# A decoder layer with woven attention: raised priority for the MLP's elementwise steps, and attention as one stream over the stages

## The chip, the cores and the metric

One core of a Trainium2 chip. The metric is the device time of one execution in microseconds. Two programs that compute the same thing are compared, one before and one after a change.

## The reference

One decoder layer on a sequence of 2048 tokens of width 1024, with a conditioning vector c. All inputs are float32.

```python
def reference(x, c, w_ada, b_ada, g_attn, w_in, b_f, sinks, w_out,
              g_mlp, w_up, conv_w, conv_b, w_down, g_final):
    mod = jax.nn.silu(c) @ w_ada + b_ada
    sh1, sc1, ga1, sh2, sc2, ga2 = jnp.split(mod, 6, axis=-1)
    for _ in range(DEPTH):
        h = modulate(rms_norm(x, g_attn), sh1, sc1)
        x = x + ga1[:, None, :] * hybrid_mixer(h, w_in, b_f, sinks, w_out)
        h2 = modulate(rms_norm(x, g_mlp), sh2, sc2)
        x = x + ga2[:, None, :] * conv_glu_mlp(h2, w_up, conv_w, conv_b, w_down)
    return rms_norm(x, g_final)
```

`modulate(h, shift, scale)` is h * (1 + scale) + shift. The mixer projects h once, runs eight heads of sliding-window attention (window 128, with ALiBi and a sink per head; "swa") and eight heads of causal forgetting attention over the whole prefix ("fox"), and projects both together. The MLP:

```python
def conv_glu_mlp(h, w_up, conv_w, conv_b, w_down):
    u = causal_dwconv(h @ w_up, conv_w, conv_b)
    a, g = jnp.split(u, 2, axis=-1)
    return (jax.nn.silu(g) * a) @ w_down
```

The inner width is 2816; the causal convolution has three taps.

## The kernel before, in words

The tokens are cut into four blocks n of 512. Every float32 product is made of three matmuls on a high and a low part (hh and hl, wh and wl): high by high, low by high, high by low. TensorE works on 128x128 weights against 512 columns (256 in parts of the attention).

For a block there are three pieces of program. `s1(n)` scales the rows of x by their RMS (`prep_tile`), transposes and modulates them (`lazy_h`) and makes q, k, v and the forget gates (products in lines L278, L611, L639). `s2(n)` is the attention of the block: scores s (L956), their running maximum mx (VectorE, L939), its transpose mt (L981) and m (L983), subtraction `t<-t,mm` (L1002), exponentials (ScalarE, L1007), the split into ph and pl (L716, L717), and the products with v (L1051, L1054). `s3(n)` is the rest:

1. the out-projection by rows (`rowmm`, L1171, operands yh, yl) in two halves of 512 columns. After each half, for each of four row tiles: gtmp = product times gate (L1245), x1row = x1row + gtmp (L1247), a store to x1_d (L1248) and the sum of squares (ScalarE, L487). After the second half the reciprocal root rs on GpSimd (L491, L492) and the scaling of both halves of the row by it on ScalarE (through `pscale`, L114, and at L1255);
2. the transposes of the scaled rows (L513), the modulation (hraw, L521, with mod and scl from the product of c and w_ada) and the split hh, hl (L114, L526). `lazy_h(rows, 8, 24, 2)` does this in two parts of 256 columns;
3. the up-projection (L1289) for 22 pairs of column tiles; a product lies in one of four PSUM tiles d. For each tile: u on ScalarE (L1319), two more taps on VectorE (L1322, L1325), the halo of the block before (L1330) and the halo for the next (ScalarE L1332, VectorE L1333), which is the last reader of the d tile. There are three u tiles. Then tanh (L1341), the product (L1342) and act (L1344);
4. the down-projection by rows (L1171, operands ah, al made by `get`, L1275 and L1276) in two halves, and the last RMS.

`merge(main, side, ratio)` weaves attention into the main work in program order: as main advances by some cost, the generator of the attention advances by ratio times that. A "B" event lets it fill a bubble, and "U" forces the fox heads of the block to be done. The stages are `s1(1)` and `s1(2)` with attention 0; `s3(0)` with attention 1; `s1(3)` and `s3(1)` with attention 2; `s3(2)` with attention 3; and `s3(3)` alone. `prime(n)` lets the first loads of an attention start in the stage before. The products of c with the later columns of w_ada (loads wada, L189; sums acc on VectorE, L201, L203) are spread over the first two stages.

The order of the instructions on each engine is set ahead of the run by a scheduler. It goes by program order as priority, and `tc.high_priority(offset=...)` moves the instructions inside it forward by so many places; among the instructions that it holds to be ready, the one with the best priority goes next. At run time every engine works through its queue strictly in that order, and DMAs are issued from SP's queue.

## Time and profile before

| | |
|---|---|
| time, median of 3 runs | 2670.57 us (2666.57 to 2671.02) |
| the profiled execution's own time | 2663.14 us |
| its span in the profile | 2661.4 us |
| mean granted TensorE clock | 0.976 |
| TensorE busy | 2544.1 us (96%), 12852 matmuls |
| VectorE, ScalarE, GpSimd busy | 1918.8, 1472.0, 91.7 us |
| HBM traffic | 588.24 MB in DMA packets, 220 GB/s over the span |

The profile shows one execution. Its times are in microseconds from the start of the span. A row of the waits names the waiting engine and line, then the engine, tile and line that ended the wait, then the sum, the count and the longest. A row of a timeline has start, duration, engine, line, operation, tiles written and read, shapes, count, and in brackets the idle time of that engine just before and what ended it. The letters are PE for TensorE (PEld for its weight loads), DVE for VectorE, ACT for ScalarE, POOL for GpSimd, SP for SyncE. Neighbouring instructions overlap a little, so eight in a row of 0.68 us each take less than eight times that.

### The profile page before, as it was taken

The page shows a single profiled execution, that of the slowest core. Times are in us where ns is not written, and L with a number is a line of the kernel's source. Part 1 is how long each engine was busy: PE and PEld are TensorE (multiplying, and loading weights), DVE is VectorE, ACT ScalarE, POOL GpSimd, SP SyncE. Part 2 cuts the span into 40 slices and gives each one's busy share as a digit, 9 for nine tenths or more (in the row PEclk, how much of TensorE's full clock was granted, in tenths as well). Part 3 has the DMA queues.
Part 4 walks back from the last instruction along what each step waited for, and adds up shares of the span by engine and source line. Part 5 has one row for each costly group of instructions (what it writes and reads, how often), then busy time and mean ns, then how long its engine had stood idle before and what let it go on. Part 6 is the DMA issues. An engine that isn't in the chain of part 4 may idle for free.

```text
span 2661.4 us, 38402 instructions
## 1 busy us (share of the span) xinstructions
PE 2544.1 (96%) x12852; PEld 2155.2 (81%) x12852; DVE 1918.8 (72%) x3813; ACT 1472.0 (55%) x3085; POOL 91.7 (3%) x171
## 2 busy tenths in 40 slices
PE   7999989799999999989999999799998999999998
PEld 5888888688887889878888888688877878888887
DVE  5568767799998668778888767888888876344433
ACT  4456665655667675575556665755555665421222
POOL 1001000100000010010000000100000000000000
PEclk9999999799999999999999999899998999999999
DMA  6967679576557876756666799365554577655564
GB/s 229 303 204 256 194 226 339 179 257 212 183 188 216 284 253 213 254 184 234 227 231 235 256 304 315 100 216 193 185 168 142 173 238 236 227 197 191 190 236 175
DMA packets 304769, 588.24 MB, mean 221 GB/s; under 512 B 32188, under 2 KB 137396, under 8 KB 304572
## 3 DMA queue, kind: packets, MB, share of 16 engines
q1 hardware_dynamic: 304572, 585.79, 65.8%
q8 instruction: 102, 1.67, 0.3%
q14 instruction: 95, 0.78, 0.1%
HBM read 440.95 MB, written 144.71 MB: 220 GB/s over the span
## 4 chain that ended last, share of the span: by engine, by line
PE 83%; DVE 5%; DMA 5%; ACT 4%; issue 2%; POOL 1%; SPq 1%; POOLq 0%; DVEq 0%; ACTq 0%
PE d L1289 36%; PE d L1171 21%; PE d L611 8%; PE s L956 4%; PE d L639 3%; PE o L1054 2%; PE o L1051 2%; PE d L278 1%; PE mb L988 1%; DVE t L1002 1%; PE s L786 1%; DMA yraw<-yd 1%; DMA q<-qd 1%; DMA wada<-in_w_ada_dram 1%; PE pt L828 1%
## 5 line engine op out<-in xcount | busy, mean ns | idle before, releaser
L1289 PE MATMUL d<-hh,wkh 128*128 128x512 f32 (+1 forms) x920 | 352.9, 386 | 13.4 <-DVE halo L1333 8.7
L1289 PE MATMUL d<-hl,wkh 128*128 128x512 f32 (+1 forms) x920 | 353.7, 386 | 0.0
L1289 PE MATMUL d<-hh,wkl 128*128 128x512 f32 (+1 forms) x920 | 352.5, 384 | 0.0
L381 DVE TENSOR_TENSOR wl<-wr,wh 128x1024 fp32r<-128x1024 f32 (+5 forms) x184 | 218.9, 1190 | 84.1 <-ACT wh L380 82.1
L973 ACT ACTIVATE t<-s,bc 128x256 f32<-128x256 f32 (+3 forms) x464 | 201.1, 483 | 135.7 <-PE s L956 72.0
L380 ACT CAST wh<-wr 128x1024 fp32r<-128x1024 f32 (+5 forms) x184 | 188.7, 1026 | 152.0 <-PE d L1289 62.8
L1319 ACT ACTIVATE u<-d,cb,cw 128x512 f32<-128x512 f32 x176 | 136.3, 777 | 207.7 <-PE d L1289 190.8
L716 ACT CAST ph<-t 128x512 fp32r<-128x512 f32 (+2 forms) x304 | 176.8, 590 | 119.3 <-PE o L1051 117.8
L1322 DVE SCALAR_TENSOR_TENSOR u<-d,cw,u 128x511 f32<-128x511 f32 x176 | 130.4, 743 | 150.7 <-ACT u L1319 149.6
L717 DVE TENSOR_TENSOR pl<-t,ph 128x512 fp32r<-128x512 f32 (+2 forms) x304 | 192.5, 644 | 31.5 <-ACT ph L716 31.2
L1289 PE MATMUL d<-hl,wh 128*128 128x512 f32 (+1 forms) x552 | 211.9, 385 | 0.0
L1289 PE MATMUL d<-hh,wh 128*128 128x512 f32 (+1 forms) x552 | 211.2, 384 | 0.4 <-ACT hh L114 0.4
L1289 PEld LDWEIGHTS d<-hh,wkh 128*128 128x128 f32 x920 | 173.9, 190 | 46.5 <-DVE halo L1333 9.3
L1289 PE MATMUL d<-hh,wl 128*128 128x512 f32 (+1 forms) x552 | 210.9, 383 | 0.0
L956 PE MATMUL s<-q,kkb 128*128 128x256 f32 (+2 forms) x1024 | 195.1, 309 | 7.3 <-ACT t L973 3.1
L1289 PEld LDWEIGHTS d<-hh,wkl 128*128 128x128 f32 x920 | 174.9, 190 | 32.0
L1289 PEld LDWEIGHTS d<-hl,wkh 128*128 128x128 f32 x920 | 174.9, 190 | 31.3 <-DVE hl L526 0.2
L1007 ACT ACTIVATE t<-t 128x512 f32<-128x512 f32 (+2 forms) x304 | 170.2, 601 | 13.0 <-DVE t L1006 10.1
L956 PEld LDWEIGHTS s<-q,kkb 128*128 128x128 f32 x1024 | 152.0, 194 | 19.9 <-ACT t L973 5.3
L1051 PE MATMUL o<-ph,vvb 128*128 128x256 f32 (+2 forms) x512 | 150.8, 310 | 10.0 <-ACT ph L716 3.6
L1054 PE MATMUL o<-pl,vvb 128*128 128x256 f32 (+2 forms) x512 | 146.7, 306 | 8.7 <-DVE pl L717 8.7
L611 PE MATMUL d<-hh,wh 128*128 128x512 f32 x360 | 142.0, 398 | 5.5 <-DVE lf L654 3.9
(232 smaller groups left out, 6078.9 us busy)
## 6 DMA issues: line engine op xcount, KB each, us to landing
wkh<-wsu SPq DMA_DIRECT2D x110, 512.0 KB, 3.3
wkl<-wsu SPq DMA_DIRECT2D x110, 512.0 KB, 4.2
wr<-in_w_up_dram SPq DMA_DIRECT2D x66, 512.0 KB, 4.8
wkh<-wsd SPq DMA_DIRECT2D x55, 512.0 KB, 3.9
wkl<-wsd SPq DMA_DIRECT2D x55, 512.0 KB, 4.3
wada<-in_w_ada_dram SPq DMA_DIRECT2D x96, 256.0 KB, 5.5
wr<-in_w_in_c_dram SPq DMA_DIRECT2D x45, 512.0 KB, 4.3
wsu<-wh SPq DMA_DIRECT2D x44, 512.0 KB, 2.9
```

What stands on the lines that cost most here:

```text
L380: nc.scalar.copy(wh, raw)
L381: nc.vector.tensor_sub(wl, raw, r32(wh))
L611: nc.tensor.matmul(ps, a[:, k, :], b[k], start=(k == 0 and i == 0), stop=(k == KT - 1 and i == 2),)
L716: nc.scalar.copy(ph[:, e0:], src[:, e0:])
L717: nc.vector.tensor_sub(pl[:, e0:], src[:, e0:], r32(ph[:, e0:]))
L956: nc.tensor.matmul(ps[:, o + low(c0) : o + w], st["kks"][kb // 4][:, (kb % 4) * P : (kb % 4 + 1) * P], qs[a][:, low(c0) : w], start=(a == ...
L973: nc.scalar.activation(tt[:, plain : o + w], ps[:, plain : o + w], AF.Identity, bias=bias(kb))
L1007: nc.scalar.activation(t1, t1, AF.Exp)
L1051: nc.tensor.matmul(po[:, c:], v, ph[:, o + c : o + w], start=(kb == 0), stop=False)
L1054: nc.tensor.matmul(po[:, c:], v, pl[:, o + c : o + w], start=False, stop=(kb == nkb - 1))
L1171: nc.tensor.matmul(acc[t], l[:, ts], r[:, k % 2, :], start=(i == 0 and l is ah and r is wh), stop=(i == n_k - 1 and l is al),)
L1289: nc.tensor.matmul(ps[:, c], w[a][:, k, :], b[k][:, c], start=(k == 0 and i == 0), stop=(k == KT - 1 and i == 2),)
```

## The change

It has four parts.

- `first()` raises the priority by 400 places for: the transposes and modulation of h2, the residual and RMS part after the second half of the out-projection, `get` (ah, al), the u and halo steps, and the gate.
- The scaling of rows by rs moves from ScalarE to VectorE: for block 0's x rows (8 instructions), and for the first half of the x1 rows (4 per block).
- The store of x1 follows the sum of squares in program order.
- The attention is one stream over the stages: the generator of the next attention is opened as soon as one ends, in the second and third stage also ahead of its own stage, and each stage's ratio is worked out from the attention still owed up to its block and the stage's length less 24. The priming hooks go.

```diff
+LEAD = 24.0
+AHEAD = 400
...
+    def first():
+        return tc.high_priority(offset=AHEAD)
...
-                a, b = h_pair(hh, hl, j)
-                ps = side_ps(w) if side else dense_ps(w)
-                transposes(ps, rows[part * nt : (part + 1) * nt], j)
-                modulate_one(a[:, c], b[:, c], ps, j, a0, s0)
+                with first() if parts == 2 else nullcontext():
+                    a, b = h_pair(hh, hl, j)
+                    ps = side_ps(w) if side else dense_ps(w)
+                    transposes(ps, rows[part * nt : (part + 1) * nt], j)
+                    modulate_one(a[:, c], b[:, c], ps, j, a0, s0)
...
-            pscale(r, r, rs)
+            if n == 0:
+                nc.vector.tensor_scalar(r, r, rs, None, ALU.mult)
+            else:
+                pscale(r, r, rs)
...
             for t in range(4):
-                tmp = tp.tile([P, 512], F32, tag="t", name="gtmp")
-                row = rows[t][half]
-                nc.vector.tensor_mul(tmp, r[t], gb)
-                adder = nc.vector
-                adder.tensor_add(row, row, tmp)
-                nc.sync.dma_start(x1_d[n][t * P : (t + 1) * P, cs], row)
-                if half == 0:
-                    sss.append(sums())
-                sumsq(row, sss[t][:, half : half + 1], tmp)
-                if half == 1:
-                    rs = rsqrt(sss[t])
-                    pscale(rows[t][0], rows[t][0], rs)
-                    nc.scalar.activation(tmp, row, AF.Copy, scale=rs)
-                    rows[t][1] = tmp
+                with first() if half == 1 else nullcontext():
+                    tmp = tp.tile([P, 512], F32, tag="t", name="gtmp")
+                    row = rows[t][half]
+                    nc.vector.tensor_mul(tmp, r[t], gb)
+                    nc.vector.tensor_add(row, row, tmp)
+                    if half == 0:
+                        sss.append(sums())
+                    sumsq(row, sss[t][:, half : half + 1], tmp)
+                    nc.sync.dma_start(x1_d[n][t * P : (t + 1) * P, cs], row)
+                    if half == 1:
+                        rs = rsqrt(sss[t])
+                        nc.vector.tensor_scalar(rows[t][0], rows[t][0], rs, None, ALU.mult)
+                        nc.scalar.activation(tmp, row, AF.Copy, scale=rs)
+                        rows[t][1] = tmp
...
+            with first():
+                if "h" in tails:
+                    ah, al = h_pair({}, {}, k, "t")
+                else:
+                    ah = tp.tile([P, TB], F32R, tag="t", name="ah")
+                    al = tp.tile([P, TB], F32R, tag="t", name="al")
+                nc.scalar.copy(ah, acts[k])
+                nc.vector.tensor_sub(al, acts[k], r32(ah))
...
+                with first():
+                    u = tp.tile([P, TB], F32, tag="u", name="u", bufs=3)
+                    c0, c1, c2 = (cw[t][:, ci : ci + 1] for t in range(3))
...
+            with first():
+                e = tp.tile([P, TB], F32, tag="t", name="e")
+                nc.scalar.activation(e, g, AF.Tanh, scale=0.5)
+                nc.vector.tensor_mul(a, a, g)
+                act = ap.tile([P, TB], F32, tag="act", name="act")
+                nc.vector.scalar_tensor_tensor(act, e, 1.0, a, ALU.add, ALU.mult)
...
+    stream = {"n": 0, "gen": None}
+
+    def attend(most):
+        while stream["n"] <= most:
+            if stream["gen"] is None:
+                stream["gen"] = s2(stream["n"])
+            try:
+                cost, need = next(stream["gen"])
+            except StopIteration:
+                fox_done.add(stream["n"])
+                stream["n"] += 1
+                stream["gen"] = None
+                continue
+            clock[0] += cost
+            stream["cost"] = stream.get("cost", 0.0) + cost
+            return cost, need
+        return None
+
+    def merge(main, n, length):
+
+        most = n if n in (0, NB - 1) else n + 1
+        begun = stream.get("cost", 0.0)
+        goal = sum(att_cost(i) for i in range(n + 1))
+        ratio = RM[n] * (goal - begun) / max(length - LEAD, 1.0)
         done_m = done_s = 0.0
         since, need = 1e9, 0.0
-        for main_event in main:
...
-                    spent += cost + (need if bubble else 0.0)
-                    clock[0] += cost
-                    since = 0.0
-                except StopIteration:
-                    side = None
-        if side is not None:
-            for cost, need in side:
-                clock[0] += cost
+            if isinstance(event, tuple) and event[0] == "U":
+                while n not in fox_done and stream["n"] <= n:
+                    got = attend(n)
+                    done_s += got[0] if got else 0.0
+            while spent < bubble or (done_s < done_m * ratio and since >= need):
+                got = attend(n if bubble > 1e6 else most)
+                if got is None:
+                    break
+                done_s += got[0]
+                need = got[1]
+                spent += got[0] + (need if bubble else 0.0)
+                since = 0.0
+        while stream["n"] <= n:
+            attend(n)
...
-    merge(s1(0), prologue_late(), 1.0)
-    merge(woven(chain(s1(1), s1(2)), late["extra"], 8), s2(0), RM[0] * att_cost(0) / 190.0)
-    merge(s3(0, [lambda: prime(2)]), s2(1), RM[1] * att_cost(1) / 383.0)
-    merge(chain(s1(3), s3(1, [lambda: yprep(2, 1), lambda: prime(3)])), s2(2), RM[2] * att_cost(2) / 478.0)
-    merge(s3(2, [lambda: yprep(3, 1)]), s2(3), RM[3] * att_cost(3) / 383.0)
-    merge(s3(3), None, 0.0)
...
+    merge(woven(chain(s1(1), s1(2)), late["extra"], 8), 0, 190.0)
+    merge(s3(0), 1, 383.0)
+    merge(chain(s1(3), s3(1, [lambda: yprep(2, 1)])), 2, 478.0)
+    merge(s3(2, [lambda: yprep(3, 1)]), 3, 383.0)
+    for event in s3(3):
+        clock[0] += event if not isinstance(event, tuple) else 0.0
```

The `with first():` blocks around u and the gate hold the same instructions as before.

How the order moves, at three places. In these rows the first number is the place in the engine's queue and a count stands at the end; lines of the changed kernel are some ten higher (L1322 becomes L1333, L1333 becomes L1344, L1002 becomes L1011).

VectorE late in the third block's up-projection, before:

```order
2649 L1061 TENSOR_TENSOR yo<-o,yo 64x256
2650 L1344 SCALAR_TENSOR_TENSOR act<-e,u 128x512
2651 L1322 SCALAR_TENSOR_TENSOR u<-d,cw_1138,u 128x511 x2
2652 L1325 SCALAR_TENSOR_TENSOR u<-d,cw_1128,u 128x510
2653 L1330 TENSOR_TENSOR u<-u,halo 128x2
2654 L1325 SCALAR_TENSOR_TENSOR u<-d,cw_1128,u 128x510
2655 L1330 TENSOR_TENSOR u<-u,halo 128x2
2656 L1002 TENSOR_TENSOR t<-t,mm 128x512 x7
2657 L1032 TENSOR_REDUCE rl<-lt 128x2
2658 L1342 TENSOR_TENSOR u<-u 128x512
2659 L933 TENSOR_TENSOR mx<-t 128x512
2660 L1333 SCALAR_TENSOR_TENSOR halo<-d,cw_1138,halo 128x1 x2
```

and after:

```order
2745 L1356 SCALAR_TENSOR_TENSOR act<-e,u 128x512
2746 L1333 SCALAR_TENSOR_TENSOR u<-d,cw_1150,u 128x511 x2
2747 L1336 SCALAR_TENSOR_TENSOR u<-d,cw_1140,u 128x510
2748 L1341 TENSOR_TENSOR u<-u,halo 128x2
2749 L1336 SCALAR_TENSOR_TENSOR u<-d,cw_1140,u 128x510
2750 L1341 TENSOR_TENSOR u<-u,halo 128x2
2751 L1011 TENSOR_TENSOR t<-t,mm 128x512 x5
2752 L1354 TENSOR_TENSOR u<-u 128x512
2753 L1011 TENSOR_TENSOR t<-t,mm 128x512 x2
2754 L1041 TENSOR_REDUCE rl<-lt 128x2
2755 L942 TENSOR_TENSOR mx<-t 128x512
2756 L1344 SCALAR_TENSOR_TENSOR halo<-d,cw_1150,halo 128x1 x2
```

Before, two u steps are followed by all their taps, then seven subtractions, then the two halos. After, at the place where this shape is left in this phase, five subtractions stand ahead of the product of the gate and two behind it, and the halos again come last.

VectorE at the start of the second block's up-projection, before:

```order
1611 L381 TENSOR_TENSOR wl<-wr,wh 128x1024
1612 L1322 SCALAR_TENSOR_TENSOR u<-d,cw_1138,u 128x511 x2
1613 L1325 SCALAR_TENSOR_TENSOR u<-d,cw_1128,u 128x510
1614 L1330 TENSOR_TENSOR u<-u,halo 128x2
1615 L983 TENSOR_REDUCE m<-mt 128x2
1616 L1325 SCALAR_TENSOR_TENSOR u<-d,cw_1128,u 128x510
1617 L1330 TENSOR_TENSOR u<-u,halo 128x2
1618 L381 TENSOR_TENSOR wl<-wr,wh 128x1024
1619 L1322 SCALAR_TENSOR_TENSOR u<-d,cw_1138,u 128x511
1620 L1342 TENSOR_TENSOR u<-u 128x512
1621 L933 TENSOR_TENSOR mx<-t 128x512
1622 L1333 SCALAR_TENSOR_TENSOR halo<-d,cw_1138,halo 128x1 x2
```

and after:

```order
1673 L386 TENSOR_TENSOR wl<-wr,wh 128x1024
1674 L1333 SCALAR_TENSOR_TENSOR u<-d,cw_1150,u 128x511 x3
1675 L1336 SCALAR_TENSOR_TENSOR u<-d,cw_1140,u 128x510
1676 L1341 TENSOR_TENSOR u<-u,halo 128x2
1677 L942 TENSOR_TENSOR mx<-t 128x512
1678 L1336 SCALAR_TENSOR_TENSOR u<-d,cw_1140,u 128x510
1679 L1341 TENSOR_TENSOR u<-u,halo 128x2
1680 L1011 TENSOR_TENSOR t<-t,mm 128x512 x6
1681 L1336 SCALAR_TENSOR_TENSOR u<-d,cw_1140,u 128x510
1682 L1341 TENSOR_TENSOR u<-u,halo 128x2
1683 L386 TENSOR_TENSOR wl<-wr,wh 128x1024
1684 L1344 SCALAR_TENSOR_TENSOR halo<-d,cw_1150,halo 128x1
```

Before, the first two halos stand behind a weight split (wl) and one maximum (mx); the subtractions come later. After, three u steps come at once, and six subtractions stand ahead of the weight split and the first halo.

VectorE at the third block's change from out- to up-projection, before:

```order
2303 L1245 TENSOR_TENSOR gtmp<-d,gb_17893 128x512 x4
2304 L1002 TENSOR_TENSOR t<-t,mm 128x512 x8
2305 L1061 TENSOR_TENSOR yo<-o,yo 64x256
2306 L1247 TENSOR_TENSOR x1row<-x1row,gtmp 128x512
2307 L933 TENSOR_TENSOR mx<-t 128x512
2308 L1247 TENSOR_TENSOR x1row<-x1row,gtmp 128x512 x3
```

and after:

```order
2330 L1255 TENSOR_TENSOR gtmp<-d,gb_18068 128x512 x4
2331 L1256 TENSOR_TENSOR x1row<-x1row,gtmp 128x512
2332 L1070 TENSOR_TENSOR yo<-o,yo 64x256
2333 L1041 TENSOR_REDUCE rl<-lt 128x2
2334 L1011 TENSOR_TENSOR t<-t,mm 128x512 x5
2335 L1256 TENSOR_TENSOR x1row<-x1row,gtmp 128x512
2336 L1011 TENSOR_TENSOR t<-t,mm 128x512 x2
2337 L942 TENSOR_TENSOR mx<-t 128x512
2338 L1256 TENSOR_TENSOR x1row<-x1row,gtmp 128x512 x2
2339 L1045 RECIPROCAL rl<-rl 128x2
2340 L1263 TENSOR_SCALAR x1row<-x1row,rs 128x512
```

Before, all four x1row sums stand behind eight subtractions. After, the first stands ahead of them, the second behind five, the last two behind seven, and the scaling of an x1row by rs has its place in VectorE's queue.

More of the change, by code (lines that the diff above doesn't have):

```diff
@@ L1079, in tile_decoder_layer @@
     clock = [0.0]
-    fox_done = [False]
+    fox_done = set()
     primed = {}
@@ L1099, in s2 @@
         held = []
-        fox_done[0] = False
         i = 0
@@ L1123, in s2 @@
                         groups = list(units[i]["groups"])
-                    fox_done[0] = i > n_fox
+                    if i > n_fox:
+                        fox_done.add(n)
             if len(held) > DEPTH or (held and not drained):
@@ L1269, in get @@
         def get(k):
-            if "h" in tails:
-                ah, al = h_pair({}, {}, k, "t")
-            else:
-                ah = tp.tile([P, TB], F32R, tag="t", name="ah")
-                al = tp.tile([P, TB], F32R, tag="t", name="al")
-            nc.scalar.copy(ah, acts[k])
-            nc.vector.tensor_sub(al, acts[k], r32(ah))
+            with first():
[6 more added lines that the diff above has]
+                nc.vector.tensor_sub(al, acts[k], r32(ah))
             return ah, al
@@ L1339, in s3 @@
                 next(extra, None)
-            e = tp.tile([P, TB], F32, tag="t", name="e")
-            nc.scalar.activation(e, g, AF.Tanh, scale=0.5)
-            nc.vector.tensor_mul(a, a, g)
-            act = ap.tile([P, TB], F32, tag="act", name="act")
-            nc.vector.scalar_tensor_tensor(act, e, 1.0, a, ALU.add, ALU.mult)
+            with first():
[4 more added lines that the diff above has]
+                nc.vector.scalar_tensor_tensor(act, e, 1.0, a, ALU.add, ALU.mult)
             acts.append(act)
@@ L1449, in chain @@
             yield from g
-    def merge(main, side, ratio):
+    stream = {"n": 0, "gen": None}
[19 more added lines that the diff above has]
+        ratio = RM[n] * (goal - begun) / max(length - LEAD, 1.0)
         done_m = done_s = 0.0
         since, need = 1e9, 0.0
-        for main_event in main:
-            bubble, cst = 0.0, main_event
-            if isinstance(cst, tuple):
-                bubble, cst = cst[1], 0.0
+        for event in main:
+            bubble, cst = 0.0, event
+            if isinstance(event, tuple):
+                bubble, cst = event[1], 0.0
             done_m += cst
@@ L1461, in merge @@
             spent = 0.0
-            if isinstance(main_event, tuple) and main_event[0] == "U":
-                while side is not None and not fox_done[0]:
-                    cost, need = next(side)
-                    done_s += cost
-                    clock[0] += cost
-            while side is not None and (
-                spent < bubble or (done_s < done_m * ratio and since >= need)
-            ):
-                try:
-                    cost, need = next(side)
-                    done_s += cost
-                    spent += cost + (need if bubble else 0.0)
-                    clock[0] += cost
-                    since = 0.0
-                except StopIteration:
-                    side = None
-        if side is not None:
-            for cost, need in side:
-                clock[0] += cost
+            if isinstance(event, tuple) and event[0] == "U":
[12 more added lines that the diff above has]
+            attend(n)
     def att_cost(n):
@@ L1505, in tile_decoder_layer @@
     late["extra"] = prologue_later()
-    merge(s1(0), prologue_late(), 1.0)
-    merge(woven(chain(s1(1), s1(2)), late["extra"], 8), s2(0), RM[0] * att_cost(0) / 190.0)
-    merge(s3(0, [lambda: prime(2)]), s2(1), RM[1] * att_cost(1) / 383.0)
-    merge(chain(s1(3), s3(1, [lambda: yprep(2, 1), lambda: prime(3)])), s2(2), RM[2] * att_cost(2) / 478.0)
-    merge(s3(2, [lambda: yprep(3, 1)]), s2(3), RM[3] * att_cost(3) / 383.0)
-    merge(s3(3), None, 0.0)
+    late_steps, since, need = prologue_late(), 0.0, 3.0
+    for event in s1(0):
+        cst = event if not isinstance(event, tuple) else 0.0
+        clock[0] += cst
+        since += cst
+        if since >= need:
+            cost, need = next(late_steps, (0.0, 1e9))
+            clock[0] += cost
+            since = 0.0
+    for _ in late_steps:
+        pass
+    merge(woven(chain(s1(1), s1(2)), late["extra"], 8), 0, 190.0)
[4 more added lines that the diff above has]
+        clock[0] += event if not isinstance(event, tuple) else 0.0
 _INS = [
```

32 lines of the change are left out of this document (15 added, 17 removed).

## The prediction

> **What bounds the kernel now.** I read the page first (share of each engine, then the chain), then the busy time in stretches of the span, then what TensorE waited for, and last the rows of VectorE around the longest waits.
>
> ```profile
> span 2661.4 us, 38402 instructions
> PE 2544.1 (96%) x12852; PEld 2155.2 (81%) x12852; DVE 1918.8 (72%) x3813; ACT 1472.0 (55%) x3085; POOL 91.7 (3%) x171
> ...
> PEclk9999999799999999999999999899998999999999
> ...
> PE 83%; DVE 5%; DMA 5%; ACT 4%; issue 2%; POOL 1%; SPq 1%; POOLq 0%; DVEq 0%; ACTq 0%
> ```
>
> TensorE is the bound: 96% busy, 83% of the chain. The change removes no matmul, so it can only win or lose time in which TensorE stands or runs at a lower clock. The stretches that hold this time:
>
> ```profile
> core 0: us, PE busy (x) PEld busy (x) DVE busy (x) ACT busy (x) POOL busy (x), PEclk, DMA share, GB/s
> 0.00:100.00 100.00, 80.22 (x386) 69.01 (x387) 52.63 (x96) 45.74 (x81) 6.82 (x19) 0.98 0.72 240
> 100.00:400.00 300.00, 289.26 (x1593) 252.80 (x1592) 209.34 (x512) 188.04 (x419) 18.37 (x40) 0.99 0.74 234
> 400.00:550.00 150.00, 131.65 (x626) 108.29 (x625) 117.84 (x217) 85.55 (x164) 10.18 (x10) 0.87 0.79 266
> ...
> 1140.00:1180.00 40.00, 31.51 (x205) 28.52 (x204) 34.88 (x72) 36.56 (x86) 10.08 (x8) 0.87 0.42 134
> ...
> 1660.00:1716.00 56.00, 41.26 (x271) 36.46 (x270) 43.97 (x84) 42.41 (x99) 7.79 (x9) 0.88 0.33 107
> ...
> 1915.00:2060.00 145.00, 129.26 (x656) 109.26 (x654) 123.46 (x246) 84.61 (x182) 0.82 (x4) 0.92 0.48 157
> 2060.00:2160.00 100.00, 92.32 (x495) 78.48 (x494) 87.06 (x174) 65.03 (x148) 0.61 (x3) 0.97 0.56 181
> ...
> 2280.00:2310.00 30.00, 25.60 (x162) 23.74 (x161) 10.72 (x23) 21.04 (x47) 2.78 (x6) 0.89 0.33 114
> ```
>
> TensorE idles 19.8 us in the first 100, 18.4 at the first block's change from out- to up-projection (400 to 550), 8.5 and 14.7 at those of the second and third, 15.7 in the third block's up-projection (1915 to 2060), 7.7 in its down-projection, 4.4 at the last block's change. A gap costs more than itself, since the granted clock falls (0.87 to 0.92 there). The chain of waits prices that, right after one gap and late in the program:
>
> ```profile
> 1927.10 6.70 PE d L1289 x21
> ```
> ```profile
> 2301.87 231.21 PE d L1289 x1030
> ```
>
> At full clock a matmul starts every 231.21 / 1030 = 0.2245 us, so 21 take 4.71; they took 6.70. A gap of about 3 us costs 2.0 more behind it.
>
> What TensorE waited for, over the span:
>
> ```profile
> PE d L513 <- ACT x1row L114: 14.5, 4, 7.6
> PE sd L513 <- ACT xrow L114: 10.0, 4, 6.3
> ...
> PE d L1289 <- DVE halo L1333: 8.7, 3, 3.3
> ...
> PE d L1171 <- ACT ah L1275: 6.9, 7, 2.4
> ```
>
> **The change, part by part.** The profiled execution took 2663.14 us (span 2661.4), 7.4 under the median of 2670.57; I sum against 2663.14 and add 7.4 back.
>
> *Third block's up-projection (raised u, halo, gate).* The three halo waits have one shape. The VectorE rows of the last:
>
> ```profile
> 2018.45 0.42 DVE L983 TENSOR_REDUCE m<-mt 128x2 f32<-128x256 f32 x1 [5.12 <-PE mt L981]
> ...
> 2020.26 0.42 DVE L1061 TENSOR_TENSOR yo<-o,yo 64x256 f32<-64x256 f32 x1 [0.48 <-ACT yo L1060]
> 2020.79 0.69 DVE L1344 SCALAR_TENSOR_TENSOR act<-e,u 128x512 f32<-128x512 f32 x1
> 2021.61 1.48 DVE L1322 SCALAR_TENSOR_TENSOR u<-d,cw,u 128x511 f32<-128x511 f32 x2
> ...
> 2024.45 4.89 DVE L1002 TENSOR_TENSOR t<-t,mm 128x512 f32<-128x512 f32 x8
> ...
> 2029.87 0.20 DVE L1333 SCALAR_TENSOR_TENSOR halo<-d,cw,halo 128x1 f32<-128x1 f32 x1
> ```
>
> VectorE idles 5.12 for the attention's m, with act queued behind it; only act frees a u tile, so two u steps come late and together, and the subtraction of the maximum (t<-t,mm, eight in a row, 4.89) goes ahead of the halos that free two of the four d tiles. Raised priority cannot shorten the idle time, as the queue's order is fixed before the run; it can put the block behind the halos. In the new order of VectorE two such spots are left in this phase: rows 2745 to 2756 (two u, then five and two subtractions, then the halos) and one at the end of the phase where seven subtractions stand ahead of both u. Elsewhere the halos come first. Three stalls become two: one gap of 8.7 / 3 = 2.9 and its 2.0, so **-4.9**. Bounds: all gone -14.7, one more +4.9.
>
> *Second block's change to the up-projection.* There the new order makes such a spot: three u steps, then six subtractions and a weight split ahead of the first halo (rows 1674 to 1684). Six subtractions at 4.89 / 8 = 0.61 are 3.7, one more tap 0.74 (half of 1.48 for two like steps); the gate's product (0.69, like act) and m (0.42) no longer stand there. So the first halo comes 3.7 + 0.74 - 0.69 - 0.42 = 3.3 us later against the u steps. TensorE did not wait there before, so the slack is unknown: the cost lies between 0 and 3.3 + 2.0 = 5.3. No row is nearer to one end, so I take half, **+2.7**.
>
> *Third block's change (raised residual and RMS part).* Before:
>
> ```profile
> 1671.36 4.90 DVE L1002 TENSOR_TENSOR t<-t,mm 128x512 f32<-128x512 f32 x8 [0.28 <-ACT mm L995]
> ...
> 1676.52 0.67 DVE L1247 TENSOR_TENSOR x1row<-x1row,gtmp 128x512 f32<-128x512 f32 x1
> 1677.11 0.67 DVE L933 TENSOR_TENSOR mx<-t 128x512 f32<-128x512 f32 x1
> ```
>
> All four x1row sums stood behind eight subtractions. Now the first stands ahead of them, the second behind five, the last two behind seven. The first transposes need the first two rows: the second row gains three subtractions and the mx step, 3 x 0.61 + 0.67 = 2.5; the last two rows gain nothing. This ends in the 7.6 us wait (the longest x1row wait), so **-2.5**; ends 0 and -7.6 - 2.0 = -9.6.
>
> *Scalings moved from ScalarE to VectorE (8 of xrow, 16 of x1row).* ScalarE's price is below; VectorE's is not in the trace, and the nearest row is its multiplication by a per-partition scalar of the same shape:
>
> ```profile
> L114 ACT ACTIVATE x1row<-x1row,rs x16: 704/722/735, 478.1 to 2288.1; 128x512 f32<-128x512 f32 x16
> ```
> ```profile
> L201 DVE TENSOR_SCALAR acc<-wada,cc x12: 457/482/487, 11.8 to 570.5; 128x512 f32<-128x512 f32 x12
> ```
>
> So 0.48 against 0.72. At the last block's change ScalarE loses 4 x 0.72 = 2.9 in a stretch where VectorE is busy 10.72 of 30 us and takes the 4 x 0.48 in its free time: between 0 and -2.9; half, **-1.4**. At the other three changes the attention keeps VectorE busy; the new wait of its queue there is a rival below, and I set it to nothing since what it holds up (attention) has been paid for by matmuls already woven in. At the start:
>
> ```profile
> 8.97 1.32 ACT L114 ACTIVATE xrow<-xrow,rs 128x512 f32<-128x512 f32 x2
> ...
> 16.03 1.34 ACT L114 ACTIVATE xrow<-xrow,rs 128x512 f32<-128x512 f32 x2 [0.83 <-POOL rs L492]
> ...
> 25.58 1.52 ACT L521 ACTIVATE hraw<-xt,mod,scl 128x512 f32<-128x512 f32 x2 [1.65 <-DVE scl L265]
> ```
>
> First and last of four pairs: ScalarE loses 4 x 1.33 = 5.3 ahead of its copies, VectorE gains 8 x 0.48 = 3.9 ahead of the sums for scl. Both chains meet at 25.58. I take the difference, **-1.4**; ends -5.3 and +3.9.
>
> *ah and al splits raised:* at most the 6.9 of the ah waits. Most are at the start of a phase, where the split waits for its input whatever its rank; **-3**, ends 0 and -6.9.
>
> *First block's change:* the longest idle stretch, and DMA is full there:
>
> ```profile
> 470.00:480.00 10.00, 5.64 (x24) 3.81 (x22) 10.00 (x18) 5.57 (x13) 1.40 (x2) 0.86 1.05 346
> 480.00:490.00 10.00, 5.62 (x26) 5.17 (x25) 10.00 (x21) 3.70 (x9) 6.05 (x5) 0.50 1.05 333
> ```
>
> VectorE is busy without a break, with the mod sums of w_ada among its work. The new SP order puts the last ten w_ada loads (2.56 MB, 7.6 us at 335 GB/s) behind the four x1d stores, which wait for the x1row sums; against that, the denser attention leaves some 5 us more of attention matmuls (by the counts between the last out-projection and first up-projection matmul, at 0.2245 for 512 columns and half for 256) to fill the gap. **0**, ends -5 and +7.6.
>
> *The stream itself:* the ratio of attention to main work rises from 0.23 to 0.27 in the first stage and falls from 0.20 to 0.19 in the third. By the order's counts the attention left when the last woven up-projection begins falls from 131 to 123 us of matmuls: 6% thinner, too little to count beside the order of single steps; 0. The first stage idles 10.7 us of 300 and has VectorE's slack to take the denser weave. Removing the priming hooks and storing x1d after the sum of squares cost nothing: each only moves a DMA whose reader is a stage away.
>
> Sum: -4.9 + 2.7 - 2.5 - 1.4 - 1.4 - 3 = **-10.5**, or 2652.6 for an execution like the profiled one, 2660 for the median.
>
> **Rivals.** *(1) Nothing gained.* The stalls begin with VectorE waiting for m, which comes from TensorE's own queue; that stays, so stalls only change place: the halo term 0, ah 0, ScalarE's relief not on the path, and +2.7 - 2.5 left. 2671. For it: two of three patterns survive in the new order.
>
> *(2) Slower: VectorE waits for GpSimd.* The scaling of x1row now stands in VectorE's queue and waits for rs; ScalarE waited before, and everything of the attention now queues behind it. GpSimd's rows:
>
> ```profile
> 1153.49 5.57 POOL L491 TENSOR_SCALAR rs<-ss 128x1 f32<-128x1 f32 x1 [2.47 <-ACT gtmp L487]
> ```
> ```profile
> 1679.00 4.02 POOL L491 TENSOR_SCALAR rs<-ss 128x1 f32<-128x1 f32 x1 [21.47 <-ACT gtmp L487]
> 1683.11 0.98 POOL L492 TENSOR_TENSOR rs<-rs,mhalf 128x1 f32<-128x1 f32 x1
> 1684.18 0.30 POOL L491 TENSOR_SCALAR rs<-ss 128x1 f32<-128x1 f32 x1
> 1684.57 0.56 POOL L492 TENSOR_TENSOR rs<-rs,mhalf 128x1 f32<-128x1 f32 x1
> ```
>
> Undisturbed a pair takes 0.86. Four rows of 0.86 + 0.48 are 5.4 per change, 16 for the three with attention, all at moments when TensorE already waits. With the 10.5 of gains that nets +5.6: 2676. It decides from about 10 us on the path. Against it: while VectorE waits, TensorE still has transposes and attention, and much of the work ahead was ready earlier. The rows 5.57 and 4.02 against 0.30 show GpSimd held up while VectorE ran without a break.
>
> The Trainium skill ("SBUF — State Buffer", Who interferes with whom) says why: GpSimd shares a port pair with VectorE, whoever issues first holds it for the instruction, and a VectorE step with two SBUF inputs blocks a GpSimd step that reads SBUF. The trace agrees (0.30 becomes 5.57). By that rule the raised sums, packed ahead of the subtractions, hold rs up as before, and the scalings queue behind it for some 4 to 5 us rather than 0.86 at each change: three times 4 more, 2688. The rows don't say that it happens once VectorE itself stands.
>
> *(3) A larger gain.* All three halo stalls (-14.7), the ah waits (-6.9), the 7.6 wait with its clock (-9.6), 5.3 at the start, none of the new stall: -36.5, 2634. For it: each has its cause among the raised steps. Against: the two patterns left.
>
> **How the numbers follow.** A measurement of this kernel (2666.57 to 2671.02) tells about 0.2%, 5.3 us, from no change. My forecast (2652 to 2665) has 0.41, (3) 0.14, (1) 0.23, (2) 0.22, of which the packed form 0.05. So faster 0.55, same 0.23, slower 0.22. The forecast is 2660; the range 2640 to 2680 leaves out the far half of (3) and the far part of (2), with the bounds of the first block's change (-5, +7.6) inside it.
>
> **What would show it.** Right: two or three halo waits of TensorE instead of three, one of them near the second block's change; the longest x1row wait near 5 us; ah waits about half; the x1row scaling on VectorE near 0.48. Wrong: halo waits gone or doubled; VectorE waiting for POOL's rs by over 10 us in sum; a longer idle stretch at the first block's change, with mod released by w_ada loads later against the x1row sums; a x1row scaling slower than 0.72.

## The result, and the profile after

The changed kernel takes 2685.68 us (median of 4, 2683.79 to 2686.64) where the kernel before takes 2668.57 on the same terms (2665.91 to 2671.02). The ratio is 1.0064, 95% interval 1.0049 to 1.0078: slower by some 17 us, where 2660 and "faster" were forecast. The profiled execution took 2683.79 us.

The page of the changed kernel, the rows that answer to those shown of before:

```profile
span 2682.1 us, 38490 instructions
## 1 busy us (share of the span) xinstructions
PE 2557.3 (95%) x12852; PEld 2163.5 (81%) x12852; DVE 1934.3 (72%) x3837; ACT 1462.2 (55%) x3061; POOL 99.0 (4%) x171
...
PEclk9999999699999999999999999899999999999999
...
PE 81%; DVE 8%; DMA 4%; ACT 3%; issue 2%; SPq 1%; POOL 1%; POOLq 0%; DVEq 0%; ACTq 0%
```

TensorE has the same matmuls and is still the bound, but 8% of the chain is VectorE's now, 5% before. What TensorE waited for:

```profile
PE o L1063 <- DVE pl L726: 17.2, 19, 2.2
PE o L1060 <- ACT ph L725: 15.0, 3, 9.6
...
PE d L1299 <- DVE halo L1344: 5.3, 2, 3.6
PE d L1180 <- ACT ah L1285: 5.3, 4, 1.9
...
PE d L518 <- DVE x1row L1263: 1.9, 4, 0.7
```

The waits for the attention's pl and ph before:

```profile
PE o L1054 <- DVE pl L717: 8.7, 12, 1.4
...
PE o L1051 <- ACT ph L716: 3.6, 3, 2.2
```

The waits that the prediction wanted gone did shrink: x1row from 14.5 to 1.9, halo from 8.7 to 5.3, ah from 6.9 to 5.3. In their place TensorE waits for the attention's own ph and pl.

Where the time went shows best by phase. For each phase I take the time from its first matmul to the next phase's first, less its matmuls at the spacing they have at full clock (0.2245 us for 512 columns, 0.119 for 256, 0.108 for 128). What is left is time in which TensorE stood or ran slowly. An up-projection begins here with its first matmul, while the last transposes of the change ahead of it are still to come; so the end of a change is booked in the up-projection. One profiled execution each, in us; the columns to the right are experiments that come below.

| phase | before | after | dense first stage alone | after, LEAD 0 | after, nothing opened ahead | after, w_ada early | scalings alone |
|---|---|---|---|---|---|---|---|
| start, to the first product | 22.8 | 21.3 | 21.6 | 21.7 | 21.8 | 21.0 | 21.5 |
| block 0 projected, then the first stage (blocks 1 and 2 projected) | 29.8 | 34.4 | 33.7 | 30.7 | 33.8 | 31.7 | 31.0 |
| block 0: out-projection and change | 31.6 | 39.1 | 38.3 | 31.0 | 39.3 | 24.5 | 31.9 |
| block 0: up-projection | 7.3 | 9.5 | 7.6 | 7.6 | 9.5 | 7.1 | 8.3 |
| block 0: down-projection, block 3 projected | 12.6 | 23.8 | 11.5 | 18.0 | 12.0 | 19.7 | 10.4 |
| block 1: out-projection and change | 7.0 | 5.7 | 7.4 | 6.6 | 11.4 | 5.7 | 7.4 |
| block 1: up-projection | 12.8 | 13.7 | 9.2 | 7.1 | 8.3 | 8.8 | 8.1 |
| block 1 down, block 2 out-projection and change | 26.9 | 23.0 | 29.1 | 17.6 | 26.0 | 23.6 | 25.2 |
| block 2: up-projection | 31.7 | 24.3 | 31.9 | 33.2 | 33.1 | 24.2 | 33.1 |
| block 2 down, block 3 out-projection and change | 25.1 | 33.6 | 24.3 | 27.6 | 27.1 | 33.0 | 21.9 |
| rest | 15.2 | 15.2 | 15.3 | 15.3 | 16.4 | 15.7 | 14.7 |

After against before: 4.6 lost in the first stage, 7.5 at the first block's change, 2.2 and 11.2 in the rest of that block. From there on gains (1.3, 3.9, 7.4) and losses (0.9, 8.5) nearly cancel. So the net loss lies ahead of the second block's change.

At the first block's change TensorE cannot go on without mod. The last out-projection matmul and mod, before and then after:

```profile
472.27 0.39 PE L1171 MATMUL d<-wh,yl 128*128 128x512 f32 x1
```
```profile
507.53 0.16 DVE L215 TENSOR_TENSOR mod<-sd,bada 128x16 f32<-128x16 f32 x1
```
```profile
474.66 0.39 PE L1180 MATMUL d<-wh,yl 128*128 128x512 f32 x1
```
```profile
525.11 0.15 DVE L220 TENSOR_TENSOR mod<-sd,bada 128x16 f32<-128x16 f32 x1
```

From matmul to mod it is 35.3 us before and 50.5 after. VectorE's groups in these stretches, before (472 to 508) and after (475 to 526), the w_ada sums and three kinds of the attention's steps (columns: operation, tiles, shapes, count; busy time and mean):

```profile
L203 DVE SCALAR_TENSOR_TENSOR acc<-wada,cc,acc 128x512 f32<-128x512 f32 x15 | 10.9, 745 | 0.0
...
L939 DVE TENSOR_TENSOR mx<-mx,t 128x512 f32<-128x512 f32 (+2 forms) x5 | 2.8, 551 | 0.0
L1017 DVE TENSOR_TENSOR acc<-acc,t 128x512 f32<-128x512 f32 (+2 forms) x5 | 2.8, 551 | 0.0
...
L717 DVE TENSOR_TENSOR pl<-t,ph 128x512 fp32r<-128x512 f32 (+2 forms) x5 | 2.7, 552 | 0.0
```
```profile
L208 DVE SCALAR_TENSOR_TENSOR acc<-wada,cc,acc 128x512 f32<-128x512 f32 x20 | 14.3, 740 | 0.0
L726 DVE TENSOR_TENSOR pl<-t,ph 128x512 fp32r<-128x512 f32 (+2 forms) x12 | 6.6, 569 | 0.0
L1026 DVE TENSOR_TENSOR acc<-acc,t 128x512 f32<-128x512 f32 (+2 forms) x10 | 5.5, 546 | 0.0
L948 DVE TENSOR_TENSOR mx<-mx,t 128x512 f32<-128x512 f32 (+2 forms) x10 | 5.4, 544 | 0.0
```

Six more sums stand ahead of mod (some 4 us; of the 15 in the row of before, one starts at 507.61, behind mod), and 9.2 us more of these attention steps. In all VectorE is busy for 31.5 us between the last out-projection matmul and mod before, and for 47.7 after. It waits for no load of w_ada there; its only waits in that stretch of the changed kernel are

```profile
DVE x1row L1263 <- POOL rs L497: 2.5, 3, 0.9
```

The experiments ask whether VectorE's queue is the cause.

### The profile page after: what moved, and what is told of

Same layout as the page of the kernel before. It is cut to its first block, busy times and chain, and to the rows that moved or that the text cites. A ratio compares the mean times of both kernels' runs of the same rounds, so it can differ in the third digit from the quotient of the medians.

```text
span 2682.1 us, 38490 instructions
## 1 busy us (share of the span) xinstructions
PE 2557.3 (95%) x12852; PEld 2163.5 (81%) x12852; DVE 1934.3 (72%) x3837; ACT 1462.2 (55%) x3061; POOL 99.0 (4%) x171
## 4 chain that ended last, share of the span: by engine, by line
PE 81%; DVE 8%; DMA 4%; ACT 3%; issue 2%; SPq 1%; POOL 1%; POOLq 0%; DVEq 0%; ACTq 0%
PE d L1299 34%; PE d L1180 22%; PE d L620 8%; PE s L965 4%; PE d L648 3%; PE o L1063 2%; PE o L1060 2%; DMA wada<-in_w_ada_dram 1%; DVE t L1011 1%; PE d L283 1%; DVE pl L726 1%; PE s L795 1%; PE pt L837 1%; PE mb L997 1%; DVE wl L386 1%
## 5 line engine op out<-in xcount | busy, mean ns | idle before, releaser
L1333 DVE SCALAR_TENSOR_TENSOR u<-d,cw,u 128x511 f32<-128x511 f32 x176 | 130.7, 745 | 160.3 <-ACT u L1330 159.9
L726 DVE TENSOR_TENSOR pl<-t,ph 128x512 fp32r<-128x512 f32 (+2 forms) x304 | 194.6, 649 | 24.0 <-ACT ph L725 20.8
L965 PE MATMUL s<-q,kkb 128*128 128x256 f32 (+2 forms) x1024 | 201.3, 315 | 9.1 <-ACT t L982 4.1
L1299 PEld LDWEIGHTS d<-hh,wkl 128*128 128x128 f32 x920 | 174.2, 189 | 31.6
L1063 PE MATMUL o<-pl,vvb 128*128 128x256 f32 (+2 forms) x512 | 149.0, 310 | 17.4 <-DVE pl L726 17.2
L1060 PE MATMUL o<-ph,vvb 128*128 128x256 f32 (+2 forms) x512 | 150.1, 308 | 15.2 <-ACT ph L725 15.0
```

The source lines that it names most:

```text
L726: nc.vector.tensor_sub(pl[:, e0:], src[:, e0:], r32(ph[:, e0:]))
L965: nc.tensor.matmul(ps[:, o + low(c0) : o + w], st["kks"][kb // 4][:, (kb % 4) * P : (kb % 4 + 1) * P], qs[a][:, low(c0) : w], start=(a == ...
L1060: nc.tensor.matmul(po[:, c:], v, ph[:, o + c : o + w], start=(kb == 0), stop=False)
L1063: nc.tensor.matmul(po[:, c:], v, pl[:, o + c : o + w], start=False, stop=(kb == nkb - 1))
L1299: nc.tensor.matmul(ps[:, c], w[a][:, k, :], b[k][:, c], start=(k == 0 and i == 0), stop=(k == KT - 1 and i == 2),)
```

## The experiments

Four kernels took the change apart first: each of its three parts that move instructions alone, and the raised priorities taken out. Moving the x1d store behind the sum of squares was not run alone: in the scheduler's order every queue of such a kernel reads word for word like before.

**Raised priorities alone.**

```diff
+    def first():
+        return tc.high_priority(offset=AHEAD)
     (around the same steps as in the change; nothing else)
```

> The kernel before with the raised priorities alone: attention woven as before, scalings on ScalarE, x1d stored as before. Theory P (the raised steps push the attention's subtractions, ph and pl back in the queues of VectorE and ScalarE, and TensorE waits for them): slower by 12 to 20 us (2681 to 2689), with the waits of the products with v (ph and pl) at some 30 us in sum instead of 12. Theory W (the loss is the new weave, the priorities bring the halo and x1row gains): faster by 5 to 12 us (2657 to 2664), ph and pl waits as before. Theory G (the scalings' wait for GpSimd): as W.

Measured: 1.0025 (1.0015 to 1.0036), 2673.66 against 2665.72. Neither number came: they cost a little, and gain nothing. x1row and halo, whose gain the prediction put down to them:

```profile
PE d L518 <- ACT x1row L116: 17.6, 4, 7.0
...
PE d L1296 <- DVE halo L1341: 6.2, 3, 3.1
```

One of the three halo waits is down to 0.5 us.

**The stream alone.**

```diff
-    merge(s3(0, [lambda: prime(2)]), s2(1), RM[1] * att_cost(1) / 383.0)
+    merge(s3(0), 1, 383.0)
     (and the rest of attend and merge as in the change)
```

> The kernel before with the attention as one stream alone: no raised priorities, scalings on ScalarE, x1d stored as before. Theory P: within 5 us of before. Theory W: slower by 15 to 25 us (2684 to 2694), with the loss where the changed kernel has it: first block's change and its down-projection, projection of the fourth block, third block's down-projection. Theory G: within 5 us of before.

Measured: 1.0098 (1.0082 to 1.0113), 2693.38 against 2665.72. The weave is the loss, all of it and more. Its x1row waits are still 15.6 us. (This edit also rewrites how the late part of the prologue is woven into block 0's projection, which the listing of the change leaves out. The runs with LEAD 0 below keep that and are faster than before, so it is not what costs.)

**Scalings on VectorE alone.**

```diff
-            pscale(r, r, rs)
+            if n == 0:
+                nc.vector.tensor_scalar(r, r, rs, None, ALU.mult)
+            else:
+                pscale(r, r, rs)
...
-                    pscale(rows[t][0], rows[t][0], rs)
+                        nc.vector.tensor_scalar(rows[t][0], rows[t][0], rs, None, ALU.mult)
```

The x1d store stands behind the sum of squares here too.

> The kernel before with the 24 scalings on VectorE and the x1d store behind the sum of squares, nothing else. Theories P and W: within 4 us of before (the start gains some 1.5). Theory G (VectorE's queue waits for rs at the three changes with attention): slower by 6 to 16 us, mostly between 400 and 550 and at the second and third block's change.

Measured: 0.9961 (0.9947 to 0.9976), 2654.22: faster by 10 us. Theory G falls, though VectorE does wait for rs:

```profile
DVE x1row L1263 <- POOL rs L497: 6.7, 9, 1.2
```

6.7 us in nine waits cost the kernel nothing that shows.

**The change without the raised priorities.**

```diff
     def first():
-        return tc.high_priority(offset=AHEAD)
+        return nullcontext()
```

> The changed kernel without the raised priorities: stream and scalings remain. Theory P: back within 5 us of before (2664 to 2674), ph and pl waits back near 12 us. Theory W: slower still than the changed kernel, 2690 to 2697, as the gains of the priorities at the halos and the third block's change are lost too. Theory G: slower by 6 to 16 us than before.

Measured: 1.0057 (1.0043 to 1.0070), 2680.69. The parts nearly add up: 0.98 - 0.39 = 0.59% for stream and scalings together. Theory P falls; of theory W the place is right, and the gains it gave to the priorities are not there.

The next four ask what in the stream costs: the ratios that LEAD raises, or the opening of the next attention ahead of its stage.

**LEAD 0.**

```diff
-LEAD = 24.0
+LEAD = 0.0
```

> The changed kernel with a LEAD of 0 in place of 24, so each stage's ratio of attention to main work is worked out over its whole length (first stage 0.23 instead of 0.27); opening the next attention ahead, the raised priorities and the scalings stay. Theory D (the loss is the denser weave that LEAD makes: in the first stage it holds up the w_ada sums and pushes their last loads behind the x1d stores, late in the third block it packs the attention): 12 to 20 us faster than the changed kernel, 2650 to 2658 where before takes 2666. Theory O (the loss is that the next attention is opened ahead and without its priming loads): no more than 4 us faster than the changed kernel.

Measured: 0.9968 (0.9956 to 0.9980), 2656.53 against 2665.99. One number turns the change from 0.64% slower to 0.32% faster.

**LEAD 0 in the first stage only.**

```diff
-        ratio = RM[n] * (goal - begun) / max(length - LEAD, 1.0)
+        ratio = RM[n] * (goal - begun) / max(length - (LEAD if n > 0 else 0.0), 1.0)
```

> The changed kernel with LEAD taken as 0 in the first stage only. Theory D: the first stage's 3 us and the first block's change's 8 come back, 8 to 12 us faster than the changed kernel; the rest of the loss stays. Theory O: within 4 us of the changed kernel.

Measured: 0.9986 (0.9975 to 0.9996). 0.78% or some 21 us come back from the first stage's ratio alone, twice what was expected. By the phases 7.6 us of it lie in the first stage, 9.2 at the first block's change, 6.7 in the rest of that block and 3.5 in block 1's up-projection (between one profiled execution of each, 26 us apart).

**Nothing opened ahead of its stage.**

```diff
-        most = n if n in (0, NB - 1) else n + 1
+        most = n
```

> The changed kernel with no attention opened ahead of its own stage (LEAD 24, raised priorities and scalings stay). Theory D: within 5 us of the changed kernel, or slower, since the later stages have more left to weave. Theory O: 8 to 15 us faster than the changed kernel, from the first block's down-projection and the fourth block's projection.

Measured: 1.0044 (1.0030 to 1.0058). Opening ahead costs where theory O says (block 0's down-projection and block 3's projection, 23.8 with it and 12.0 without), but block 1's change and block 2's up-projection lose 30.0 with it and 44.5 without; over all phases 5 us are left. Net 0.2%, with intervals that overlap.

**Stream with LEAD 0 and the scalings, priorities out.**

```diff
-LEAD = 24.0
+LEAD = 0.0
...
-        return tc.high_priority(offset=AHEAD)
+        return nullcontext()
```

> Stream with LEAD 0 and the scalings on VectorE, without the raised priorities. Theory D together with the runs so far (priorities alone cost 0.25%, scalings alone gain 0.39%): the fastest so far, 2650 to 2658 where before takes 2666. Theory O: 2672 to 2680.

Measured: 0.9964 (0.9950 to 0.9979), 2653.97. The scalings alone gave 0.9961: with LEAD 0 in every stage the stream as such costs and wins nothing measurable.

**The dense first stage alone, on the kernel before.**

```diff
-    merge(woven(chain(s1(1), s1(2)), late["extra"], 8), s2(0), RM[0] * att_cost(0) / 190.0)
+    merge(woven(chain(s1(1), s1(2)), late["extra"], 8), s2(0), RM[0] * att_cost(0) / 166.0)
```

> The kernel before with one number changed: the first stage's ratio of attention to main work 44/166 (0.27, as LEAD makes it) in place of 44/190 (0.23). Theory D: the denser first stage is enough by itself, slower by 5 to 12 us (2671 to 2678 where before takes 2666), in the first stage and the first block's change. Rival D2 (the dense first stage costs only where the stream's next stage follows it): within 4 us of before.

Measured: 1.0043 (1.0030 to 1.0057), 2674.95 against 2663.18. Enough by itself, and in the two phases named: 29.8 to 33.7 and 31.6 to 38.3. So it is not the stream that is needed for this loss, but the ratio. In the changed kernel the ratio costs more (some 21 us against 12), in block 0's later phases and block 1's up-projection too; why was not taken apart.

**x1d stores off SP's queue.**

```diff
-                    nc.sync.dma_start(x1_d[n][t * P : (t + 1) * P, cs], row)
+                    (nc.scalar if n == 0 and half == 1 else nc.sync).dma_start(
+                        x1_d[n][t * P : (t + 1) * P, cs], row
+                    )
```

> The changed kernel with the four x1d stores of block 0's second half issued from ScalarE's queue, so SP's queue doesn't hold the last ten w_ada loads behind them. Theory Q (the loads wait in SP's queue for the x1row sums): 6 to 9 us faster than the changed kernel, mod earlier by about 8 us against the out-projection's end. Theory V (the loads come late because VectorE, busy with attention, frees their tiles late): within 3 us of the changed kernel.

Measured: 1.0080 (1.0067 to 1.0093), no gain. SP's last rows ahead of the change, with the stores gone from them:

```profile
486.58 0.71 SPq L194 DMA_DIRECT2D wada<-in_w_ada_dram  x1
488.69 0.33 SPq L426 DMA_DIRECT2D wr<-in_w_up_dram  x1
490.09 9.72 SPq L194 DMA_DIRECT2D wada<-in_w_ada_dram  x10
```

The ten loads still go out from 490 on, and mod comes at 524.17. My bound of +7.6 at this place came near the 7.5 lost by luck: its cause was another. Theory Q falls.

**Scalings of block 0's x rows alone, and of the x1 rows alone.**

```diff
-            pscale(r, r, rs)
+            (as above, for n == 0)
```

> The kernel before with only the 8 scalings of block 0's x rows on VectorE. Both theories: the start gains 1.3 us as in the run with all 24, the rest nothing: 1 to 3 us faster than before.

```diff
-                    pscale(rows[t][0], rows[t][0], rs)
+                    nc.vector.tensor_scalar(rows[t][0], rows[t][0], rs, None, ALU.mult)
```

> The kernel before with only the 16 scalings of x1 rows on VectorE. Theory S (the waits for x1row, 14.5 us in sum, go): 7 to 10 us faster than before, in the changes from out- to up-projection. Theory R (the gain is that the queues after them come out in another order): 7 to 10 us faster too, but in the down-projections, the changes no more than 2 us faster each.

Measured: 0.9992 (0.9979 to 1.0005) and 0.9974 (0.9965 to 0.9983). The 16 x1 scalings hold most of the gain. By the rows of the table the changes gain little (31.6 to 31.1, 7.0 to 7.6), block 1's up-projection 4.7 and the phase that holds block 2's down-projection 4.6, which looks like theory R. But the table books the end of a change in the up-projection. Taken from the first out-projection matmul to the 96th of the up-projection, where the transposes are done, the second, third and last change gain 5.3, 3.8 and 2.3 us, and the first loses 1.4. The three down-projections together gain less than 1 us. So theory S holds for the place. At the second change GpSimd's rs step, 5.57 us before, is now

```profile
1152.82 2.37 POOL L491 TENSOR_SCALAR rs<-ss 128x1 f32<-128x1 f32 x1 [2.12 <-ACT gtmp L487]
```

It ends at 1155.19. VectorE's run of steps ends at 1155.10, since the next one waits for rs:

```profile
1155.88 0.49 DVE L1254 TENSOR_SCALAR x1row<-x1row,rs 128x512 f32<-128x512 f32 x1 [0.78 <-POOL rs L492]
```

TensorE's wait for hraw there falls from 3.2 us to 0.3. That the freed GpSimd step is what wins at the other two changes is not shown.

**w_ada loads and sums earlier, dense first stage kept.** The loads of w_ada were tied behind the last weight load; now they are free, and in the first of the two kernels the sums are raised as well.

```diff
-            with behind():
+            with nullcontext():
                 nc.sync.dma_start(w, w_ada[i, k])
-            ada_step(acc, w, k)
+            with tc.high_priority(offset=400):
+                ada_step(acc, w, k)
```

> The changed kernel, dense first stage and all, with the w_ada loads no longer tied behind the weight loads and the w_ada sums raised by 400: from the first gtmp of the second half to mod VectorE's queue then holds 14.9 us of attention and 16 sums, where the changed kernel has 20.2 and 21, and the kernel before 13.7 and 16 (counted in the order, at 0.60 us for 512 columns). Theory V (mod comes late because of what VectorE has queued ahead of it): the first block's change loses 6 to 10 us less, the kernel is 6 to 14 us faster than the changed one. Rival T (the loss at that change is the attention that TensorE has packed there, whatever releases mod): 4 us at most.

> The changed kernel with the w_ada loads no longer tied behind the weight loads, sums not raised: 18.5 us of attention and 16 sums ahead of mod. Theory V: in between, mod some 2 to 4 us earlier against the out-projection's end, 2 to 6 us faster than the changed kernel. Rival T: within 3 us of it.

Measured: 0.9977 (0.9965 to 0.9990) and 1.0021 (1.0010 to 1.0033), from 1.0064 with neither. With both, mod comes at

```profile
502.21 0.16 DVE L221 TENSOR_TENSOR mod<-sd,bada 128x16 f32<-128x16 f32 x1
```

30.2 us after the last out-projection matmul, earlier than in the kernel before; the change loses 24.5 us where it lost 39.1. With the loads freed alone mod comes 36.2 us after that matmul, 14 us earlier than in the changed kernel where 2 to 4 were expected, and the change loses some 28. So the count of the queue was off in size, but in two doses the loss follows mod, and theory V holds: what VectorE has queued ahead of mod sets it. Rival T falls: the dense weave stays, and of the 14.6 us gained at the change the attention's matmuls there account for 2.6 (17.4 to 14.8 us at the spacing above). About half of the whole gain comes with freeing the loads alone.

**The same without the MLP's raised priorities.**

```diff
     def first():
-        return tc.high_priority(offset=AHEAD)
+        return nullcontext()
```

> The run with the early w_ada sums and loads (dense first stage, stream, scalings), with the raised priorities of the MLP taken out again. Three pairs so far had the raised priorities cost 0.25%, 0.07% and 0.04%. If they are a cost here too: 0.9955 to 0.9977 of before, the fastest or as fast as the fastest so far. If they pay once mod is no longer late: 0.9985 to 1.002.

Measured: 1.0008 (0.9993 to 1.0024). Here the priorities pay 0.31%. Over four pairs they did +0.25, +0.07, +0.04 and -0.31%, the two in the middle within the noise: no constant sign. What they do depends on the order around them. Of what they save here, 4.8 us lie in block 1's up-projection, where without them TensorE waits 3.7 us for a halo; the rest stays open.

## Why the prediction was wrong

**The step that failed** is the one called *The stream itself*, and with it the 0 at the *First block's change*. It said that the first stage "has VectorE's slack to take the denser weave". Alone the stream costs 0.98%, some 26 us. VectorE was counted by its busy share over 300 us, but what mattered was its order: the attention went in ahead of the w_ada sums, six more of them stood behind the last out-projection matmul, and mod, for which TensorE has no substitute, came 15 us later. Of the loss in the changed kernel that is the shown cause of the 7.5 us at the first block's change; the runs with LEAD 0, with the dense stage alone and with the sums early bracket it from three sides. The 4.6 us in the first stage itself come with the ratio too (33.7 with the dense stage alone), by a way that I did not take apart. The next piece, the first block's down-projection with block 3's projection (+11.2), goes away when nothing is opened ahead (12.0), but the time is then lost again later. That phase holds 58.1 us of the attention's matmuls where it held 48.1, and 45.2 with nothing opened ahead.

What I weighed was the third block's attention, 6% thinner and "too little to count beside the order of single steps"; in the first stage 0.03 in a ratio was enough to change that order. Nor was the 6% nothing. By the traces the 131 us are 80.4 in block 2's up-projection and 50.8 in the phase behind it, the 123 are 77.3 and 45.6, and the phase that has 5.2 us less loses 8.5 more (25.1 to 33.6). With LEAD 0 in every stage it has 50.8 and loses 27.6; with LEAD 0 in the first stage alone it has 45.6 and loses 33.3. All eight kernels with 45.6 to 47.0 us there lose 33.0 to 36.8, all nine with 50.8 lose 20.5 to 29.2. That the missing attention leaves TensorE's waits unfilled is the likely reason, but is not shown.

**The halo term** (-4.9, three stalls to two): in block 2's up-projection one was left, 1.7 us long (the other of the two halo waits, 3.6, is the new stall below), and that phase gained 7.4. But not for the reason given. With the raised priorities alone three halo waits remain (6.2 us), and the phase loses 34.0. With the stream alone no halo wait is left in it, and it loses 26.7. So it was the weave that took them away, and the next phase lost more than was gained (25.1 to 33.6). Rival (1), that stalls only change place, was right in this.

**The new stall at block 1's change** (+2.7) is there, at the place read from the order: six subtractions, a weight split, then the halo.

```profile
1222.64 3.70 DVE L1011 TENSOR_TENSOR t<-t,mm 128x512 f32<-128x512 f32 x6
...
1226.98 1.23 DVE L386 TENSOR_TENSOR wl<-wr,wh 128x1024 fp32r<-128x1024 f32 x1
1228.12 0.22 DVE L1344 SCALAR_TENSOR_TENSOR halo<-d,cw,halo 128x1 f32<-128x1 f32 x1
```

TensorE waits 3.6 us for it, and from its 96th matmul on that up-projection loses 10.2 us where it lost 4.3: 5.9 more, beyond my bound of 5.3. The wait is there without the raised priorities too (3.7), and gone with LEAD 0 in the first stage.

**The scalings**: VectorE's price was right:

```profile
L1263 DVE TENSOR_SCALAR x1row<-x1row,rs x16: 475/486/488, 492.7 to 2309.6; 128x512 f32<-128x512 f32 x16
```

0.486 where 0.48 was read from the neighbouring row. The start gained 1.5 (-1.4 forecast). But -2.8 for both places was too small: alone they gain 10.4 us. I set the three changes with attention to nothing; two of them gain 5.3 and 3.8 with the x1 scalings alone. The x1row wait goes from 14.5 to 2 us or less in every kernel with this part, and stays at 14.5 to 17.6 in every kernel without.

**The ah term** was -3 and the wait lost 1.6. **The third block's change** was -2.5. Its phase gained 3.9, but in block 1's down-projection, which stands ahead of the change (7.7 to 4.0); the change itself, to the end of its transposes, gained 0.6 (21.4 to 20.8), as much without the raised priorities (20.8), and with them alone it lost 3.0 (24.4). A new wait stands in it. TensorE's longest wait of the whole run, and GpSimd and ScalarE under it:

```profile
1710.92 0.58 PE L1060 MATMUL o<-ph,vvb 128*128 128x256 f32 x1 [9.63 <-ACT ph L725]
```
```profile
1702.12 6.32 POOL L496 TENSOR_SCALAR rs<-ss 128x1 f32<-128x1 f32 x1 [10.67 <-ACT gtmp L492]
```
```profile
1709.12 0.72 ACT L1264 ACTIVATE gtmp<-x1row,rs 128x512 f32<-128x512 f32 x1 [6.21 <-POOL rs L497]
1709.75 0.61 ACT L1016 ACTIVATE t<-t 128x512 f32<-128x512 f32 x1
1710.27 0.60 ACT L725 CAST ph<-t 128x512 fp32r<-128x512 f32 x1
```

The rs step, 0.30 undisturbed, takes 6.32 while VectorE runs its subtractions and sums; ScalarE stands 6.2 us at the scaling by rs with the attention's exponentials queued behind it. The Trainium skill's rule on the shared port pair ("SBUF — State Buffer", Who interferes with whom) would have it so, and the trace agrees in this row. That rs is held up is what **rival (2)** said, but at ScalarE's queue, and the scalings on VectorE are not its cause. The stream alone, with every scaling on ScalarE, has the same step:

```profile
1696.05 6.31 POOL L496 TENSOR_SCALAR rs<-ss 128x1 f32<-128x1 f32 x1 [10.68 <-ACT gtmp L492]
```

With LEAD 0 it takes 2.63. VectorE's own waits for rs at the x1 rows were 11.1 us in thirteen, over the 10 that I had named, yet the scalings alone are among the fastest: rival (2)'s price was too high by all of it. Its packed form asked what happens once VectorE itself stands; the row of 2.37 above shows a GpSimd step that ends as VectorE comes to its own wait for rs.

The forecast gave 0.22 to slower, and none of it to the weave.

## What to carry to other kernels

When side work is woven into a stage more densely, look first for what else that engine owes by a fixed time, and count what stands ahead of it in the queue: here attention steps that slipped in ahead of a few sums, on an engine that was busy 70% of the stage, held up everything behind them, and a ratio of 0.27 instead of 0.23 cost more than the whole rest of the change won. A busy share over a stage says nothing about that; the queue between the last free work and the awaited result does. And a gain at a stall in one phase is a gain only if the phases after it don't pay it back: add up the lost time over all of them, and see that the phases begin and end where the work does.

## What the runs showed of the hardware

One step on 128 single elements of GpSimd took 6.32 us in the changed kernel and 5.57 before, against 0.30 undisturbed, each time while VectorE ran without a break. It ended as that run ended: at 1708.44 against 1708.34 in the changed kernel, at 1159.06 against 1159.04 before. With the x1 scalings on VectorE, which then comes sooner to a step that itself waits for rs, the 5.57 became 2.37. In the changed kernel VectorE's own waits for rs at the x1 rows were 1.2 us at most (4.6 for the x rows at the start), ScalarE's was 6.2.
